# Strassen-Winograd sums taken in another order: S3 and T3 first and in place, one sum ahead of each product

## The chip, the cores and the metric

The kernel runs on one core of a Trainium2 chip. The metric is the device time of one execution in microseconds (us), lower is better; the time given for a kernel is the median of its runs. The engines are named as the profile names them: PE is TensorE's matmuls, PEld its weight loads, DVE is VectorE, ACT is ScalarE, POOL is GpSimd, SP is SyncE, which here issues nearly all transfers (DMA).

## The reference

One block of a streaming encoder on x of 1024 tokens by 1024 features, all in float32: a SwiGLU feed-forward, a mixing layer of two gated branches (retention and pooling), a second feed-forward.

```python
h = x + 0.5 * swiglu(rmsnorm(x, g1), w1_in, w1_out)          # 1024 -> 2 x 2816 -> 1024
u = rmsnorm(h, g2)
q, k, v, g_ret, p, gate_r, gate_p = split(u @ w_in)          # 1024 -> 7 x 1024
...                                                          # retention, pooling
merged = sigmoid(gate_r) * (ret @ w_ret_up) + sigmoid(gate_p) * (pool * scale)
h = h + merged @ w_out
h = h + 0.5 * swiglu(rmsnorm(h, g3), w2_in, w2_out)
out = rmsnorm(h, g)

def swiglu(x, w_in, w_out):
    gate, up = split(x @ w_in, 2)
    return (silu(gate) * up) @ w_out
```

## The kernel before

**A matrix product.** Every float32 number is split into a high part (a cast on ACT, L164, rounded to the matmul's format) and a low part (a subtraction on DVE, L165). One tile product is three matmuls, L184 (high by high), L185 and L186 (`mm3`). The low part of the moving weight is first read by L186, that of the operand by L185.

**A group.** Large products are done in groups of one 2x2 block of weights, with seven products in place of eight (Strassen-Winograd, function `strassen`). The weight blocks are L11, L12, L21, L22, the operand blocks R11, R12, R21, R22. The products are, with their numbers in the code, 0: L11·R11, 1: S2·T2, 2: S1·T1, 3: S3·T3, 4: L12·R21, 5: S4·R22, 6: L22·T4. The S are sums of weight blocks, the T of operand blocks. One product is 4 operand tiles of 128x512 with 3 matmuls each, so 12 matmuls. The two raw tiles of a group (`ra` with L11 and L12, `rb` with L21 and L22) are loaded by SP into a ring of 4 (`raw`). Sums that need a place of their own take a tile of a ring of 8 (`c2`). The split weight of one product is a tile of a ring of 5 (`wt`), named for its product: `wS1`, `wL22`.

**Results.** A group fills three banks: `a` (L11·R11, then + L12·R21), `b` and `e`. Product 0 goes into `a` and is copied by ACT into `b` (L529) before product 4 may add to `a`. Product 1 adds to `b`; ACT copies that to the tile `v` (L534) before product 2 may add to `b`. Product 3 goes into `e`, copied to `p7` (L551) before product 6 adds there. So in some orders PE waits for a copy that stands in ACT's row.

**Order.** `Flow.run` takes the products one after the other and prepares the weights (`prep_w`) four products ahead; behind each product it lets a few steps of background work run (operand sums, norms, gates). Groups run in pairs, A and B by turns. Where the operands are only just being made (the first pair of each feed-forward, the merge groups, w_out), the products follow `BY_OPERAND`. Engines run their instructions in the order of the program. Class `Next` makes the operands of the next stage: `r11`, `r21`, `r22`, `t1` to `t4_`, with the gain of the norm (`g`) folded in; there are four objects of it with such sums, `first` (first feed-forward), `mix` (the seven projections), `up` (retention's way up), and those of the output projection and the second feed-forward (made with `after`, which lists what each product needs).

**Names in the profile.** `a` and `a_..` are groups of the first feed-forward, `q0`, `k0`, `t1`, `p1` and so on of the projections, `ru0` to `ru3` of retention's way up, `wo0` to `wo3` of w_out, `c_..` of the second feed-forward. `n1T`, `ruT`, `mgT`, `n3T` are split T operands (in the listings of rows below `n1T12` is T1 of tile 2, `ruT40` T4 of tile 0), `n1R` and so on split R operands. `xs` are tiles of x in token order that ACT squares (L1147) for the first norm; `n1v` (L240), `n1r` (L241) are steps of its inverse root; `pg` (L1483) takes the pooling branch out of the two sum banks that `ru0b` and `ru1b` take next. `L390` and `L392` are the sums T4, `L359` T1, `L351` and `L353` T2 and T3, `L492` S1 and S2, `L505` S3, `L509` S4.

Of the kernel before, what the change touches and what calls it, by code (L numbers as in the profile page):

```python
# [15 lines left out]
ADD, SUB, MUL = ALU.add, ALU.subtract, ALU.mult  # L16
# [24 lines left out]
V_FFN1, V_MIX, V_FFN2, V_FINAL, V_SCALE, V_B0, V_B1, V_ONE = (i * KT for i in range(8))  # L41
# [9 lines left out]
N_MV, N_T4, N_RAW, N_WT, N_TL, N_C2 = 28, 9, 4, 5, 4, 8  # L51
LOOK = 4

BY_OPERAND = (0, 4, 1, 3, 2, 6, 5)


class Flow:
# [33 lines left out]
def block_kernel(ctx: ExitStack, tc, x, x_tok, x_two, vecs, f1_in, f1_out, w_in, w_v, pool_w, w_ret, w_pool, w_o,  # L91
# [3 lines left out]
    tt = nc.vector.tensor_tensor  # L95
    stt = nc.vector.scalar_tensor_tensor
# [3 lines left out]
    flow = Flow()  # L100
# [19 lines left out]
    def raw(name):  # L120
        return sb.tile([P, S], F32, tag="raw", bufs=N_RAW, name=name)
# [7 lines left out]
    def c2(name):  # L129
        return sb.tile([P, H], F32, tag="c2", bufs=N_C2, name=name)  # L130
# [4 lines left out]
    def sum_bank(name):  # L135

        return ps.tile([P, H], F32, tag="sum", bufs=N_SUM, name=name)

    def load(dst, src):
        nc.sync.dma_start(dst, src)  # L140
# [11 lines left out]
    def half(t, j):  # L152
        return t[:, j * H : (j + 1) * H]
# [22 lines left out]
    def weights(src, name, at=0):  # L176
        w = wt(name, at)
        n = src.shape[-1] // P
        split(flat(w, 0, n), flat(w, 1, n), src)
        return w  # L180
# [7 lines left out]
    def parts(m, at=slice(None)):  # L188
        return m[:, 0, at], m[:, 1, at]
# [31 lines left out]
    for n in range(N_SUM):  # L221
        b = sum_bank(f"set{n}")
# [57 lines left out]
    class Norm:  # L280
# [4 lines left out]
        def __init__(self, name):  # L285
            self.name, self.ssq, self.seen = name, None, set()
# [18 lines left out]
    class Next(Norm):  # L305

        turns = True

        def __init__(self, name, gain, keep=None):
            super().__init__(name)  # L310
            self.gain, self.keep = gain, keep
            self.M, self.Y, self.made, self.ready, self.tiles, self.t1s, self.rb = {}, {}, {}, set(), {}, {}, None
            self.t3s = set()
# [52 lines left out]
                self.t3s.add(i)  # L366

        def t2(self, i):
            self.sum1(i)
            R11, R22 = self.tiles[i, 0], self.tiles[i + 4, 1]  # L370
            self.less(R11, R22, self.t1s[i], i)
            self.put("T2", i, R11)

        def t1(self, i):
            self.put("T1", i, self.t1s[i], self.g(i))

        def t3(self, i):
            self.sum3(i)
            self.put("T3", i, self.tiles[i, 1])
# [98 lines left out]
    def strassen(nx, wa, wb, name, evac, end, begin=None, shared=(), dest=None):  # L478

        t = {}

        def blocks():
            ra, rb = raw(f"{name}ra"), raw(f"{name}rb")
            load(ra, wa)
            load(rb, wb)
            t.update(L11=half(ra, 0), L12=half(ra, 1), L21=half(rb, 0), L22=half(rb, 1))

        def combine(n, a, b, op):  # L490
            t[n] = c2(f"{name}{n}")
            tt(t[n], t[a], t[b], op)  # L492

        def prep_w(n):
            def go():
                if n == "L11":
                    blocks()
                elif n in ("S2", "S3") and "S1" not in t:
                    combine("S1", "L21", "L22", ADD)
                if n == "S2":  # L500
                    combine("S2", "S1", "L11", SUB)
                elif n == "S3":

                    t["S3"] = t["L21"]
                    tt(t["S3"], t["L11"], t["L21"], SUB)  # L505
                if n == "S4" or 3 in shared and n == "S1":

                    t["S4"] = t["S2"]
                    tt(t["S4"], t["L12"], t["S2"], SUB)  # L509
                t["w", n] = weights(t[n], f"{name}w{n}")  # L510

            return go

        def prod(dst, w, m, start, stop):
            for i in range(4):
                mm3(t[dst], parts(t["w", w], i), moving(nx.operand(m, i)), start and i == 0, stop and i == 3)

        def u(n):
            t[n] = c2(f"{name}{n}")
            return t[n]  # L520

        def b1():
            if begin:
                begin()
            t["a"] = bank(f"{name}a")
            prod("a", "L11", "R11", True, False)
            t["b"] = sum_bank(f"{name}b")
            with soon():
                copy(t["b"], t["a"])  # L529

        def b6():
            prod("b", "S2", "T2", False, False)
            with soon():
                copy(u("v"), t["b"])  # L534

        def fourth():

            if "b5" in t and "p7" in t:
                with soon():
                    evac((1, 1), t["b"], t["p7"])  # L540

        def b5():
            prod("b", "S1", "T1", False, False)
            t["b5"] = True
            fourth()

        def b7():
            t["e"] = bank(f"{name}e")
            prod("e", "S3", "T3", True, False)
            with soon():  # L550
                copy(u("p7"), t["e"])  # L551
            fourth()

        def b2():
            prod("a", "L12", "R21", False, True)
            with soon():
                evac((0, 0), t["a"], None)

        def b3():
            prod("b", "S4", "R22", False, True)  # L560
            with soon():
                evac((0, 1), t["b"], None)

        def b4():
            prod("e", "L22", "T4", False, True)
            with soon():
                evac((1, 0), t["e"], t["v"])

        def last(f):
            def go():  # L570
                f()
                t["ends"] = t.get("ends", 0) + 1
                if t["ends"] == 2:
                    end()

            return go

        g = Group([(prep_w("L11"), b1), (prep_w("S2"), b6), (prep_w("S1"), b5), (prep_w("S3"), b7),
                   (prep_w("L12"), b2), (prep_w("S4"), last(b3)), (prep_w("L22"), last(b4))])
        g.t, g.name, g.dest = t, name, dest  # L580
        g.finish = {3: last(lambda: evac((0, 1), t["b"], dest((0, 1)))), 2: lambda: evac((0, 0), t["a"], dest((0, 0)))}
        return g
# [168 lines left out]
    def ffn_in(nx, w, ops, name, ahead, start=None):  # L751
# [76 lines left out]
        if start:  # L828

            return chain(group(0), pairs_of_both(nx, (group(g) for g in order[1:]), BY_OPERAND, 3, ahead))  # L830
        return pairs_of_both(nx, (group(g) for g in order), BY_OPERAND, 2, ahead)

# [288 lines left out]
    first = Next("n1", V_FFN1)  # L1121
# [16 lines left out]
    quarters(1, range(4, 8))  # L1138
    load(cst, consts)
    flow.add(lambda: copy(ones_r, ones))  # L1140
    first.work(first.r11, first.r21, first.r12, first.r22, first.p22, first.t2, first.t3, first.t1, first.t4_)
    x_sums = eights("x_sums")

    def x_square(t):
# [9 lines left out]
    h1, h2 = spill("h1", KT), spill("h2", KT)  # L1154
# [17 lines left out]
        flow.rate = 2  # L1172
        yield from ffn_out(first, ops1, ops_done["a"], f1_out, x_two, "b", mix.quarter, end1, fetched)

    mix = Next("n2", V_MIX, h1)

    def end1(part):
        mix.work(*{2: (mix.r11,), 5: (mix.r22, mix.p22), 3: (mix.t2, mix.t1, mix.t3)}.get(part, ()))
# [551 lines left out]
    up = Next("ru", None)  # L1730
# [4 lines left out]
    def take(kts):  # L1735
        for kt in kts:
            r = t4(f"ret{kt}")
            load(r, ret[kt])
            up.tiles.update({(kt, j): half(r, j) for j in range(2)})
        if 7 in kts:  # L1740
            up.work(up.r22, up.t2, up.t1, up.t3, up.r21, up.p22, *[up.r22] * 3, up.t4_)
        else:
            up.work(up.r11)

# [47 lines left out]
    mg = Next("mg", None)  # L1792
    def after(nx):

        def t2(i):
            if i not in nx.t1s:
                nx.r22(i)
            nx.t2(i)

        return {0: nx.r11, 4: nx.r21, 1: t2, 3: nx.t3, 2: nx.t1, 6: nx.t4_, 5: nx.p22}  # L1800

    def two_groups(z):

# [76 lines left out]
    def handed(nx, last):  # L1880

        f = after(nx)

        def between(pair, n):
            if n in (3, 5):
                flow.add(*waiting)
                waiting.clear()
            if pair == 0:
                if n == BY_OPERAND[-1]:
                    flow.add(*(lambda m=m, i=i: m(i) for i in range(2) for m in (nx.r22, nx.sum1, nx.sum3)))  # L1890
                return
            flow.add(*(lambda i=i: f[n](i) for i in range(2)))

            for m in {3: (0,), 6: (4,)}.get(n, ()):
                flow.add(*(lambda i=i: f[m](i) for i in range(2, 4)))
            if n == BY_OPERAND[-1]:
                rest = [lambda m=m, i=i: f[m](i) for m in (1, 3, 2, 6, 5) for i in range(2, 4)]
                last(rest)

        return between  # L1900

    def merge():
        yield from two_by_two(two_groups(0) + two_groups(1), BY_OPERAND, handed(mg, lambda rest: flow.add(*rest)))
        yield from two_by_two((out_group(i) for i in range(4)), BY_OPERAND,
                              handed(ffn2, lambda rest: (flow.add(*rest[:4]), ffn2.stats(between=rest[4:]))))
# [198 lines left out]
```

## Time and profile before

| | |
|---|---|
| median of 3 runs | 2062.79 us (2062.39 to 2063.97) |
| the profiled execution | 2064.95 us, of which the span of the profile is 2063.2 us |
| granted TensorE clock | 0.999 |
| PE busy | 2043.0 us, 99% of the span |
| PEld busy | 1810.8 us, 88% |
| DVE busy | 1831.6 us, 89% |
| ACT busy | 1091.8 us, 53% |
| 16 DMA engines | 308 MB on the main queue, 44% |

A line of the timeline reads: start in us, duration in us, engine, line of the code and operation, out<-in (ring numbers left out), form, how many in a row, and in brackets the idle time of the engine just before and what ended it. A line of the waits reads: who waited, for whom, us in total, times, the longest. A line of the windows reads: the stretch, its length, then busy us and instructions of PE, PEld, DVE, ACT, POOL, then the granted clock, the share of the DMA engines and GB/s.

### The profile page before, as it was taken

To read this page: it belongs to the slowest core of one execution; us is meant where nothing else is said; L and a number is where in the kernel's file an instruction comes from. 1 tells how busy PE (TensorE), PEld (TensorE's weight loads), DVE (VectorE), ACT (ScalarE), POOL (GpSimd) and SP (SyncE) were. 2 spreads that over 40 slices of the span, in tenths; PEclk is the share of its full clock that TensorE was granted. 3 is DMA by queue.
4 is the path that set the end of the run, shared out by engine and by line. 5 is a ranking of instruction groups with operands and counts; after the bars stand their busy time and mean duration, and the time that the engine had idled before them with its cause. 6 is when DMAs were issued, how large, how long until landed. Compare 5 with 4: busy or idle time off the path is not lost.

```text
span 2063.2 us, 29735 instructions
## 1 busy us (share of the span) xinstructions
PE 2043.0 (99%) x10672; PEld 1810.8 (88%) x10672; DVE 1831.6 (89%) x3253; ACT 1091.8 (53%) x2064; POOL 9.0 (0%) x14
## 2 busy tenths in 40 slices
PE   9999999999999999999999999999999999999998
PEld 7888999988888888888888999888889999998887
DVE  8889898998996798989788888999989989899896
ACT  8545444554653554454447753457645545455454
POOL 0000000000000000000000000010000000000000
PEclk9999999999999999999999999999999999999999
DMA  6332424586543333243336566645223232367642
GB/s 244 137 103 77 143 87 143 200 272 197 188 144 101 114 131 115 82 153 118 118 138 231 190 223 224 237 106 169 82 91 132 93 136 88 134 208 273 212 146 100
DMA packets 120260, 313.57 MB, mean 152 GB/s; under 512 B 13361, under 2 KB 17585, under 8 KB 120113
## 3 DMA queue, kind: packets, MB, share of 16 engines
q1 hardware_dynamic: 118096, 308.01, 44.0%
q0 software_dynamic: 1440, 2.62, 0.9%
q8 instruction: 83, 1.36, 0.3%
q10 hardware_dynamic: 576, 1.05, 0.1%
q14 instruction: 65, 0.52, 0.1%
HBM read 220.93 MB, written 90.70 MB: 151 GB/s over the span
## 4 chain that ended last, share of the span: by engine, by line
PE 84%; DVE 9%; DMA 3%; ACT 3%; issue 1%; SPq 0%; ACTq 0%; DVEq 0%
PE c_b L184 2%; PE c_b L185 2%; PE c_b L186 2%; PE a_b L184 2%; PE a_b L186 2%; PE a_b L185 2%; PE c_e L186 2%; PE c_e L184 2%; PE c_e L185 2%; PE a_e L186 2%; PE a_e L184 2%; PE a_e L185 2%; PE a_a L186 1%; PE a_a L185 1%; PE a_a L184 1%
## 5 line engine op out<-in xcount | busy, mean ns | idle before, releaser
L184 PE MATMUL c_b<-n3T,c_wS 128*128 128x512 f32 x176 | 66.8, 380 | 1.7 <-ACT n3T L164 1.7
L185 PE MATMUL c_b<-n3T,c_wS 128*128 128x512 f32 x176 | 66.8, 380 | 0.0
L186 PE MATMUL c_b<-n3T,c_wS 128*128 128x512 f32 x176 | 66.7, 379 | 0.0
L184 PE MATMUL a_b<-n1T,a_wS 128*128 128x512 f32 x168 | 63.7, 379 | 0.0
L185 PE MATMUL a_b<-n1T,a_wS 128*128 128x512 f32 x168 | 63.7, 379 | 0.0
L186 PE MATMUL a_b<-n1T,a_wS 128*128 128x512 f32 x168 | 63.7, 379 | 0.0
L184 PE MATMUL a_a<-n1R,a_wL 128*128 128x512 f32 x120 | 45.5, 379 | 0.0
L185 PE MATMUL a_a<-n1R,a_wL 128*128 128x512 f32 x120 | 45.5, 379 | 0.0
L186 PE MATMUL a_a<-n1R,a_wL 128*128 128x512 f32 x120 | 45.5, 379 | 0.0
L184 PE MATMUL c_a<-n3R,c_wL 128*128 128x512 f32 x112 | 42.7, 381 | 0.7 <-ACT c_b L529 0.5
L185 PE MATMUL c_a<-n3R,c_wL 128*128 128x512 f32 x112 | 42.4, 379 | 0.0
L186 PE MATMUL c_a<-n3R,c_wL 128*128 128x512 f32 x112 | 42.4, 379 | 0.0
L184 PEld LDWEIGHTS c_b<-n3T,c_wS 128*128 128x128 f32 x176 | 33.3, 189 | 6.7 <-ACT n3T L164 2.1
L185 PEld LDWEIGHTS c_b<-n3T,c_wS 128*128 128x128 f32 x176 | 33.3, 189 | 4.8 <-DVE n3T L165 0.3
L186 PEld LDWEIGHTS c_b<-n3T,c_wS 128*128 128x128 f32 x176 | 33.3, 189 | 4.7
L186 PEld LDWEIGHTS a_b<-n1T,a_wS 128*128 128x128 f32 x168 | 31.8, 189 | 4.5
L184 PEld LDWEIGHTS a_b<-n1T,a_wS 128*128 128x128 f32 x168 | 31.8, 189 | 4.4
L185 PEld LDWEIGHTS a_b<-n1T,a_wS 128*128 128x128 f32 x168 | 31.8, 189 | 4.4
L165 DVE TENSOR_TENSOR a_wS<-a_S,a_wS 128x512 fp32r<-128x512 f32 x45 | 31.0, 690 | 3.6 <-ACT a_wS L164 3.6
L165 DVE TENSOR_TENSOR c_wS<-c_S,c_wS 128x512 fp32r<-128x512 f32 x46 | 31.7, 690 | 2.6 <-ACT c_wS L164 2.6
L164 ACT CAST a_wS<-a_S 128x512 fp32r<-128x512 f32 x45 | 27.4, 621 | 11.8 <-PE a_a L186 6.1
L184 PE MATMUL c_e<-n3T,c_wS 128*128 128x512 f32 x88 | 33.5, 380 | 0.0
(3165 smaller groups left out, 8025.3 us busy)
## 6 DMA issues: line engine op xcount, KB each, us to landing
c_ra<-in_f_in SPq DMA_DIRECT2D x22, 512.0 KB, 3.7
c_rb<-in_f_in SPq DMA_DIRECT2D x22, 512.0 KB, 3.6
a_ra<-in_f_in SPq DMA_DIRECT2D x21, 512.0 KB, 3.8
a_rb<-in_f_in SPq DMA_DIRECT2D x21, 512.0 KB, 3.7
t<-au SPq DMA_DIRECT2D x11, 512.0 KB, 3.0
b<-ag SPq DMA_DIRECT2D x11, 512.0 KB, 4.2
r<-au SPq DMA_DIRECT2D x11, 512.0 KB, 3.7
bra<-in_f_out SPq DMA_DIRECT2D x11, 512.0 KB, 5.1
```

The costliest lines, as they stand in the source:

```text
L164: copy(hi, src)
L165: tt(lo, src, hi.bitcast(F32), SUB)
L184: mm(dst, w[0], m[0], start=start, stop=False, skip_group_check=True)
L185: mm(dst, w[0], m[1], start=False, stop=False, skip_group_check=True)
L186: mm(dst, w[1], m[0], start=False, stop=stop, skip_group_check=True)
```

## The change

Weights: S3 = L11 - L21 is made first, in L11's place; then S2 = L22 - S3 in the same place, S1 = L21 + L22 in L21's place, S4 = L12 - S2 in S2's place. There are four sums of 128x512 for each group as before, but each product now has one of its own ahead of it (before, S1 and S2 were made together ahead of the first of them), and none takes a tile of `c2`. So `ra` holds S4 until it has been split.

Operands of `first`, `up`, of w_out and of the second feed-forward: T3 = R12 - gR22 in place, T2 = gR11 + T3 in place, T1 = R22 - T2 in a `c2` tile. There are three sums for each tile as before. T1 is now a plain split (L164, L165) in place of a scaled one (L168, L169). `mix` keeps the old sums.

Order: `BY_OPERAND` has product 3 (S3·T3) ahead of product 1 (S2·T2), and the lists of operand work follow it.

```diff
-BY_OPERAND = (0, 4, 1, 3, 2, 6, 5)
+BY_OPERAND = (0, 4, 3, 1, 2, 6, 5)
...
         def t2(self, i):
-            self.sum1(i)
             R11, R22 = self.tiles[i, 0], self.tiles[i + 4, 1]
-            self.less(R11, R22, self.t1s[i], i)
+            if self.by_t3:
+                self.sum3(i)
+                T3 = self.tiles[i, 1]
+                if self.gain is None:
+                    tt(R11, R11, T3, ADD)
+                else:
+                    stt(R11, R11, self.g(i), T3, MUL, ADD)
+            else:
+                self.sum1(i)
+                self.less(R11, R22, self.t1s[i], i)
             self.put("T2", i, R11)
 
         def t1(self, i):
-            self.put("T1", i, self.t1s[i], self.g(i))
+            if self.by_t3:
+                R22, T2 = self.tiles[i + 4, 1], self.tiles[i, 0]
+                t1 = c2(f"{self.name}t1{i}")
+                tt(t1, R22, T2, SUB)
+                self.put("T1", i, t1)
+            else:
+                self.put("T1", i, self.t1s[i], self.g(i))
...
-                elif n in ("S2", "S3") and "S1" not in t:
-                    combine("S1", "L21", "L22", ADD)
-                if n == "S2":
-                    combine("S2", "S1", "L11", SUB)
                 elif n == "S3":
-
-                    t["S3"] = t["L21"]
+                    t["S3"] = t["L11"]
                     tt(t["S3"], t["L11"], t["L21"], SUB)
+                elif n == "S2":
+                    t["S2"] = t["S3"]
+                    tt(t["S2"], t["L22"], t["S3"], SUB)
+                elif n == "S1":
+                    t["S1"] = t["L21"]
+                    tt(t["S1"], t["L21"], t["L22"], ADD)
...
-    first.work(first.r11, first.r21, first.r12, first.r22, first.p22, first.t2, first.t3, first.t1, first.t4_)
+    first.work(first.r11, first.r21, first.r12, first.r22, first.p22, first.t3, first.t2, first.t1, first.t4_)
...
-    mix = Next("n2", V_MIX, h1)
+    mix = Next("n2", V_MIX, h1, False)
...
-            up.work(up.r22, up.t2, up.t1, up.t3, up.r21, up.p22, *[up.r22] * 3, up.t4_)
+            up.work(up.r22, up.t3, up.t2, up.t1, up.r21, up.p22, *[up.r22] * 3, up.t4_)
...
-        return {0: nx.r11, 4: nx.r21, 1: t2, 3: nx.t3, 2: nx.t1, 6: nx.t4_, 5: nx.p22}
+        return {0: nx.r11, 4: nx.r21, 1: nx.t2, 3: t3, 2: nx.t1, 6: nx.t4_, 5: nx.p22}
```

Three places show what this does to the rows of the engines. The line numbers of the changed kernel are 8 to 15 higher for the same step (L529 becomes L541, L534 L546, L1147 L1159, L390 L405).

The first is ACT in the first pair of the first feed-forward (groups `a11` and `a1`), at the casts of T1 (`n1T10` to `n1T13`). Before:

```order
L164 CAST n1T33_621<-x3_95 128x512
L168 ACTIVATE n1T10_641<-n1t10_471,vec_66 128x512
L534 COPY a11_v_614<-a11_b_519 128x512
L164 CAST a1_wS1_624<-a1_S1_527 128x512
L168 ACTIVATE n1T11_644<-n1t11_493,vec_66 128x512
L168 ACTIVATE n1T12_665<-n1t12_521,vec_66 128x512
L168 ACTIVATE n1T13_668<-n1t13_549,vec_66 128x512
L534 COPY a1_v_639<-a1_b_547 128x512
```

And after:

```order
L1159 ACTIVATE xs6_809,x_sums_123<-xs6_809 128x1024
L1159 ACTIVATE xs7_812,x_sums_123<-xs7_812 128x1024
L563 COPY a1_p7_629<-a1_e_616 128x512
L164 CAST a11_wL22_641<-a11_rb_394 128x512
L788 COPY ag1_579<-a1_a_522 128x512
L164 CAST n1T10_633<-n1t10_631 128x512
L164 CAST n1T11_638<-n1t11_636 128x512
L546 COPY a11_v_656<-a11_b_512 128x512
L164 CAST a1_wL22_668<-a1_rb_421 128x512
L241 ACT_TABLE_LOAD
L241 ACTIVATE n1r0_832<-n1v_831 128x8
L164 CAST n1T12_660<-n1t12_658 128x512
```

The casts of T1 now stand behind the last squares of `xs` and, from `n1T12` on, behind the load of the root's table; before, they stood ahead of both.

The second is ACT in the projections, at the copy `t1v` of group `t1` (`p1ws..` are weights that the pair p1, t1 shares). Before:

```order
L164 CAST p1wx3_7151<-p1S2_7037 128x512
L1257 ACTIVATE t0z11_7148<-t0B_6890,vec_66 128x512
L164 CAST p1ws123_7157<-p1s123_7154 128x512
L551 COPY t1p7_7173<-t1e_7160 128x512
L164 CAST p1ws343_7177<-p1S2_7037 128x512
L534 COPY t1v_7192<-t1b_7055 128x512
```

And after:

```order
L1269 ACTIVATE t0z11_7098<-t0B_6844,vec_66 128x512
L563 COPY t1p7_7123<-t1e_7110 128x512
L164 CAST p1wx3_7101<-p1ra_6874 128x512
L164 CAST p1ws123_7107<-p1s123_7104 128x512
L546 COPY t1v_7142<-t1b_7006 128x512
```

The copy `t1v` no longer stands behind the second shared cast, `p1ws343`.

The third is ACT in the first pair of retention's way up, at the copy `ru1b`. Before:

```order
L529 COPY ru0b_12965<-ru0a_12952 128x512
L164 CAST ru1wS2_12979<-ru1S2_12977 128x512
L529 COPY ru1b_12999<-ru1a_12986 128x512
L164 CAST ru0wS3_13010<-ru0rb_12770 128x512
L164 CAST ruT40_13192<-ret4_12612 128x512
L164 CAST ruT41_13199<-ret5_12614 128x512
```

And after:

```order
L164 CAST ru1wS3_12881<-ru1ra_12720 128x512
L164 CAST ruT40_13098<-ret4_12522 128x512
L164 CAST ruT41_13105<-ret5_12524 128x512
L541 COPY ru1b_12901<-ru1a_12888 128x512
L164 CAST ru0wS2_12914<-ru0ra_12679 128x512
```

The casts of two T4 operands moved ahead of the copy `ru1b`. The sums that they wait for stand on DVE, after, as follows (L1495 is `pg`, L405 T4):

```order
L1495 TENSOR_TENSOR pg70_12648<-pu7d0_12765,pg70_12648 128x512
L1495 TENSOR_TENSOR pg71_12649<-pu7d1_12766,pg71_12649 128x512
L165 TENSOR_TENSOR ru0wS3_12839<-ru0ra_12679,ru0wS3_12839 128x512
L517 TENSOR_TENSOR ru1rb_12721<-ru1rb_12721 128x512
L514 TENSOR_TENSOR ru0ra_12679<-ru0rb_12680,ru0ra_12679 128x512
L405 TENSOR_TENSOR ret4_12522<-ret4_12522,ret0_12514 128x512
L405 TENSOR_TENSOR ret5_12524<-ret5_12524,ret1_12516 128x512
```

The second sum T4 is the fifth row behind `pg`, which in the kernel before was all that the copy `ru1b` waited for.

More of the change, by code (lines that the diff above doesn't have):

```diff
@@ L307, in block_kernel, with __init__ @@
         turns = True
-        def __init__(self, name, gain, keep=None):
+        def __init__(self, name, gain, keep=None, by_t3=True):
             super().__init__(name)
+            self.by_t3 = by_t3
             self.gain, self.keep = gain, keep
@@ L488, in blocks @@
             t.update(L11=half(ra, 0), L12=half(ra, 1), L21=half(rb, 0), L22=half(rb, 1))
-        def combine(n, a, b, op):
-            t[n] = c2(f"{name}{n}")
-            tt(t[n], t[a], t[b], op)
         def prep_w(n):
@@ L1793, in after, with t3 @@
     def after(nx):
-        def t2(i):
-            if i not in nx.t1s:
+        def t3(i):
+            if i not in nx.t3s:
                 nx.r22(i)
-            nx.t2(i)
-        return {0: nx.r11, 4: nx.r21, 1: t2, 3: nx.t3, 2: nx.t1, 6: nx.t4_, 5: nx.p22}
+            nx.t3(i)
+        return {0: nx.r11, 4: nx.r21, 1: nx.t2, 3: t3, 2: nx.t1, 6: nx.t4_, 5: nx.p22}
     def two_groups(z):
@@ L1884, in between @@
         def between(pair, n):
-            if n in (3, 5):
+            if n in (1, 5):
                 flow.add(*waiting)
@@ L1889, in between @@
                 if n == BY_OPERAND[-1]:
-                    flow.add(*(lambda m=m, i=i: m(i) for i in range(2) for m in (nx.r22, nx.sum1, nx.sum3)))
+                    flow.add(*(lambda m=m, i=i: m(i) for i in range(2) for m in (nx.r22, nx.sum3)))
                 return
             flow.add(*(lambda i=i: f[n](i) for i in range(2)))
-            for m in {3: (0,), 6: (4,)}.get(n, ()):
+            for m in {1: (0,), 6: (4,)}.get(n, ()):
                 flow.add(*(lambda i=i: f[m](i) for i in range(2, 4)))
             if n == BY_OPERAND[-1]:
-                rest = [lambda m=m, i=i: f[m](i) for m in (1, 3, 2, 6, 5) for i in range(2, 4)]
+                rest = [lambda m=m, i=i: f[m](i) for m in (3, 1, 2, 6, 5) for i in range(2, 4)]
                 last(rest)
```

## Prediction

> **What bounds the kernel.** I read the page's busy times first, then what PE waited for, then the timeline around each of those waits. The busy times:
>
> ```profile
> PE 2043.0 (99%) x10672; PEld 1810.8 (88%) x10672; DVE 1831.6 (89%) x3253; ACT 1091.8 (53%) x2064; POOL 9.0 (0%) x14
> ```
>
> PE is the bound, and neither its matmuls nor their shapes change. So time moves only through the 20.2 us of the 2063.2 us span in which PE is idle, or through new idle time. From the list of PE's waits, those at steps that the change touches:
>
> ```profile
> PE c_b L184 <- ACT n3T L164: 1.7, 1, 1.7
> ...
> PE t1b L184 <- ACT t1v L534: 0.9, 1, 0.9
> ...
> PE ru1a L184 <- ACT ru1b L529: 0.8, 1, 0.8
> ...
> PE wo0e L186 <- DVE wo0wS L165: 0.2, 1, 0.2
> ...
> PE t1e L186 <- DVE t1wS L165: 0.2, 1, 0.2
> ```
>
> With wo2a (1.2) and c_a (0.5) below they make 5.5 us; each costs some 0.3 us more than its gap, which counts from the end of the matmul before (0.38 long, though the next normally starts 0.22 behind it, by 165.41 us for 759 matmuls in the stretch below), and the first one after it takes 0.48. About 7.5 us is therefore all that can be won. Slower has no such bound. The difference that a measurement of this kernel can tell from none is 0.2%, 4.1 us.
>
> **Cost of the sums themselves.** Four weight sums a group before and after, three operand sums a tile: 0.6 us of DVE each (two of `pg` below take 1.28, each 0.69 long), the same number. T1's split loses a scale, which shortens it on both engines if anything (a scaled cast is 0.65 below, a plain one 0.62): nothing. What counts is order, and a place for place walk of the new rows with the old durations gives four terms.
>
> **Term 1, first feed-forward, first pair: +2.1 us.** T1 is now made last, from T2, and the casts of `n1T10` to `n1T13` stand behind the squares of `xs`.
>
> ```profile
> L140 SPq DMA_DIRECT2D xs<-in_x_tok x8: 328/328/384, 16.8 to 50.9; - x8
> L1147 ACT ACTIVATE xs<-xs x8: 1044/1056/1072, 27.1 to 55.7; 128x1024 f32<-128x1024 f32 x8
> ...
> DMA to landing us min/median/max: 3.5/4.0/8.6
> ```
>
> ```profile
> 43.75 1.95 ACT L168 ACTIVATE n1T<-n1t,vec 128x512 fp32r<-128x512 f32 x3
> 57.37 1.28 ACT L241 ACT_TABLE_LOAD   x1
> 50.48 0.38 PE L184 MATMUL a_b<-n1T,a_wS 128*128 128x512 f32 x1
> ```
>
> Before, T1 was cast by 45.7, 4.8 us before PE's third T1 tile at 50.48; the last square came at 55.7. After, all eight squares stand ahead. Two `xs` tiles alternate, so a square comes no sooner than the square two back, plus 1.1 for that square, plus a landing of 3.5 to 4.0: about 5 us a step. The first stands at 28.1 (27.1, and two T3 casts now ahead of it; casts and copies of ACT follow each other by 0.5, as three do from 741.03 to 742.55 below), so the seventh is at 43.3 and the eighth, one square and a short wait behind, at 45.3, ending at 46.4. Behind it two copies and a cast (1.5), two T1 casts (1.0), the copy `a11_v` and a cast (1.0), the table (1.28) and the root (0.2): `n1T12` is cast from 51.4 to 52.0. PE, held 0.26 by the copy `a11_v`, wants it at 50.7 and loses 1.3; DVE's low part follows at 52.7, when L185 would stand at 52.2: 0.5 more. Ends: 0, if the loads land at once, and 4, if each of three steps takes 0.6 more. I take 2.1, with the median landing.
>
> **Term 2, projections, t1: -1.2 us.** ACT, DVE and PE there:
>
> ```profile
> 736.41 0.69 DVE L165 TENSOR_TENSOR t1wS<-t1S,t1wS 128x512 fp32r<-128x512 f32 x1 [0.85 <-ACT t1wS L164]
> 738.66 0.69 DVE L165 TENSOR_TENSOR t1wS<-t1S,t1wS 128x512 fp32r<-128x512 f32 x1 [0.35 <-ACT t1wS L164]
> 740.52 0.42 DVE L593 TENSOR_TENSOR p1s<-p1s,p1S 128x256 f32<-128x256 f32 x1
> 741.03 0.62 ACT L164 CAST p1ws<-p1s 128x512 fp32r<-128x512 f32 x1 [0.40 <-DVE p1s L593]
> 742.55 0.59 ACT L534 COPY t1v<-t1b 128x512 f32<-128x512 f32 x1
> 743.19 0.48 PE L184 MATMUL t1b<-n2T,t1wS 128*128 128x512 f32 x1 [0.90 <-ACT t1v L534]
> ```
>
> After, the two half sums follow the split of 738.66 directly (done at 740.0, not 740.9), and the copy stands right behind the cast `p1ws123`: 740.6 to 741.1, before PE is free at 742.1. That takes back 1.2 us. The S3 split that `t1e` waited for stands two rows earlier on DVE, which would be 0.4 more; but late next is the S2 split of t1 at 736.41, whose cast stands behind the same rows of ACT as before, and PE would wait for that instead. Ends: 0 and -1.6; I take -1.2, for the rows leave nothing else in the copy's way.
>
> **Term 3, retention's way up: +4.2 us at ru1a, then given back.**
>
> ```profile
> 1311.77 1.28 DVE L1483 TENSOR_TENSOR pg<-pu7d,pg 128x512 f32<-128x512 f32 x2
> 1312.54 0.57 ACT L529 COPY ru1b<-ru1a 128x512 f32<-128x512 f32 x1 [0.58 <-DVE pg L1483]
> 1317.29 0.62 ACT L164 CAST ruT<-ret 128x512 fp32r<-128x512 f32 x1 [3.65 <-DVE ret L390]
> 1313.16 0.48 PE L184 MATMUL ru1a<-ruR,ru1wL 128*128 128x512 f32 x1 [0.76 <-ACT ru1b L529]
> ```
>
> Before, ACT copied `ru1b` and then waited 3.65 us for T4. After, two T4 casts stand ahead of the copy. With `pg` where it was, DVE's next rows are a split (1312.97), S1, S2 and two T4 sums, the last from 1315.4 to 1316.1; ACT casts it until 1316.7 and copies until 1317.3. PE goes on at 1317.3, not 1313.16: 4.15 us. Queued behind the copy on ACT are only splits that PE wants after that. Ends: 0 (if T4 were ready) and 5 (if DVE is two sums later there).
>
> **Term 4, w_out and the start of the second feed-forward: -4.9 us.**
>
> ```profile
> 1300.00:1470.00 170.00, 165.41 (x759) 142.39 (x758) 165.07 (x271) 101.16 (x180) 8.84 (x10) 1.00 0.49 149
> ```
>
> ```profile
> 1320.18 0.69 DVE L1837 TENSOR_TENSOR ru0h<-ru0a,rg 128x512 f32<-128x512 f32 x1
> 1419.42 0.68 DVE L492 TENSOR_TENSOR wo2S<-wo2S,wo2ra 128x512 f32<-128x512 f32 x1
> 1420.19 0.62 ACT L164 CAST wo2wS<-wo2S 128x512 fp32r<-128x512 f32 x1 [1.41 <-PE wo3a L186]
> 1421.35 0.48 PE L184 MATMUL wo2a<-mgR,wo2wL 128*128 128x512 f32 x1 [1.24 <-ACT wo2b L529]
> 1458.42 0.48 PE L184 MATMUL c_a<-n3R,c_wL 128*128 128x512 f32 x1 [0.54 <-ACT c_b L529]
> 1468.15 0.48 PE L184 MATMUL c_b<-n3T,c_wS 128*128 128x512 f32 x1 [1.74 <-ACT n3T L164]
> ```
>
> In this stretch DVE is as full as PE, 165 of 170 us, and PE's waits are DVE's lateness handed on: the copy `wo2b` stood behind the cast of S2, whose sum ended at 1420.11 (the PE row in that bracket is the last of several semaphores, but `wo3a` had nothing to do with the sum). After, the first sum, S3, stands about nine rows earlier, and the wait goes (-1.5). DVE's splits run a few rows ahead of PE, and its evacuation of `ru0a` at 1320.18 stood 8 us behind PE, which had ended that product by 1312.4 (ru1a's 1313.16 less the gap), so 4.2 us of PE's delay at ru1a does not delay DVE: PE arrives later at wo0e, c_a and c_b (0.4, 0.8 and 2.1 with the spread matmuls), and finds them ready. DVE by itself delivers the low T3 part that the second feed-forward waits for at 1467.7; PE without waits, 4.8 less and 4.2 more than before, wants it at 1468.3. So terms 3 and 4 make -0.7 together; without the delay at ru1a the same place would be DVE's, at -1.0. Ends: +4.2, if DVE is delayed with PE, and -4.9. I take -0.7, since both ways of counting meet there.
>
> **What I cost at nothing.** The `ra` tile is held until S4 and its half sums are split.
>
> ```profile
> 1651.00 0.33 SPq L140 DMA_DIRECT2D c_ra<-in_f_in  x1
> ...
> 1659.80 0.69 DVE L165 TENSOR_TENSOR c_ws<-c_S,c_ws 128x512 fp32r<-128x512 f32 x1 [0.41 <-ACT c_ws L164]
> ...
> 1668.52 0.68 DVE L165 TENSOR_TENSOR c_wL<-c_ra,c_wL 128x512 fp32r<-128x512 f32 x1
> ```
>
> ```profile
> c_ra<-in_f_in SPq DMA_DIRECT2D x22, 512.0 KB, 3.7
> ```
>
> The next pair's first load was issued at 1651.0; after, it waits for the split of 1659.8, goes out at 1660.5, lands after 3.7 at 1664.2, and is first split at 1668.5: 4.3 us to spare. If that cover were gone, every pair would lose what is missing. The diagonal of the second norm's spread (`n20b`) and T1 of tiles 2 and 3 in the second feed-forward come within 0.5 us of PE: +0.2 for both.
>
> **The sum.** +2.1 - 1.2 - 0.7 + 0.2 = +0.4 us on the profiled execution. That execution took 2064.95 us, 2.2 above the median of the runs; I apply the difference to the median: 2063.2 us.
>
> **A rule of the skill against this.** At ru1a PE would be idle for 5.0 us, where its longest idle time now is 1.7 at a granted clock of 1.00. The Trainium skill, "TensorE: Matmul & The Clock Gate", Part 1 on the clock gate, says that an idle window of about 3.4 us halves the array's clock until it has been busy as long. No row here shows it. By the page's figure some 1.7 us would be added, an estimate, and the sum would be 2064.9.
>
> **Rivals.**
> *The held tiles make loads late* (slower). The rows for it: SP issues in order, and DVE already waits for `c_ra` in the timeline of each pair. Against it: 4.3 us to spare. It decides once a landing takes over 8 us, against 3.7. With 22 groups, 11 pairs, in this feed-forward and as many in the first, 0.4 us a pair would be 8.8 us, and with my sum 2072.0. Chance 0.12.
> *The delays add and nothing comes back* (slower): DVE's evacuations wait on PE after ru1a, so the waits of w_out and c_b stay. +2.1 - 1.2 + 4.2 + 0.2 = +5.3: 2068.1. The point is whether DVE's idle time between 1320 and 1400 grows. Chance 0.10.
> *The delays do not come* (faster): DVE is ahead at T4 and the squares land early, while term 4 holds with DVE's limit loosened by the smoother sums: -1.2 - 4.9 = -6.1: 2056.7; it must win c_b's 2.1 too to pass 4.1. Chance 0.12.
> *PE runs at half pace after the idle 5 us*: one product of 12 matmuls at 0.44, not 0.22, us: +2.6, 2065.8. Chance 0.08.
> *The delay of term 1 fails to come, the rest holds* (the loads land while ACT is busy anyway): -1.7, 2061.1. Chance 0.13.
> My forecast, between 2061.5 and 2065: 0.45.
>
> **Numbers.** Faster by over 0.2%: 0.12. Slower: 0.20, the first two rivals less the mild end of the second. The rest, 0.68, is the same. The range takes in the second rival and most of the third: 2057.8 to 2068.4.
>
> **What the profile after would show.** Term 1: a wait of a_b for `n1T` of 1.5 to 2 us near 51. Term 2: no row t1b <- t1v. Term 3: ru1a <- ru1b near 5 us. Term 4: no wait at wo2a, and none over 1 us at c_a and c_e or c_b. I am wrong if groups beyond the first pairs show PE waits for weights, or DVE waits for `ra` longer than before.

## Result and the profile after

The changed kernel takes 2073.33 us (median of 6 runs, 2070.26 to 2075.35); the kernel before, run beside it, 2063.97 us (median of 6, 2062.39 to 2064.91). The ratio is 1.0046, with a 95% interval of 1.0036 to 1.0056: slower by 9.4 us, where 2063.2 us and a range up to 2068.4 us had been predicted.

The page's busy times of the changed kernel; the profiled execution took 2070.26 us, its fastest, with a span of 2068.5 us:

```profile
PE 2044.4 (99%) x10672; PEld 1810.2 (88%) x10672; DVE 1835.1 (89%) x3253; ACT 1092.7 (53%) x2064; POOL 9.1 (0%) x14
```

The same instructions, nearly the same busy times, and PE idle for 24.1 us instead of 20.2. What PE waited for at the steps in question (total us, times, longest):

```profile
PE ru1a L184 <- ACT ru1b L541: 3.1, 1, 3.1
...
PE c_e L185 <- DVE n3T L165: 1.0, 2, 0.7
PE a_b L184 <- ACT n1T L164: 1.0, 1, 1.0
PE a_b L184 <- ACT a_v L546: 1.0, 1, 1.0
...
PE dp6b L185 <- DVE dp6m L165: 0.6, 2, 0.4
PE bp6b L185 <- DVE bp6m L165: 0.6, 2, 0.4
...
PE c_a L184 <- ACT c_b L541: 0.5, 1, 0.5
...
PE wo0b L186 <- DVE wo0wS L165: 0.5, 1, 0.5
PE wo1b L186 <- DVE wo1wS L165: 0.4, 1, 0.4
PE t1b L186 <- DVE t1wS L165: 0.4, 1, 0.4
```

wo2a, t1b at the copy, and c_b at `n3T` are gone, as forecast (`n3T` is now waited for by c_e); a_b and ru1a are there, as forecast. bp6b and dp6b, the second products of the two down projections, are new, and stood nowhere in the prediction. What DVE waited for shows why:

```profile
DVE ds L931 <- DMA dL22a<-in_f_out: 2.4, 1, 2.4
...
DVE bs L931 <- DMA bL22a<-in_f_out: 2.0, 1, 2.0
```

At T1 near 50 and at ru1a the rows behind PE's waits are these (ACT first, then PE):

```profile
46.51 1.06 ACT L1159 ACTIVATE xs<-xs 128x1024 f32<-128x1024 f32 x1 [1.53 <-DMA xs<-in_x_tok]
52.60 1.12 ACT L164 CAST n1T<-n1t 128x512 fp32r<-128x512 f32 x2
53.26 0.48 PE L184 MATMUL a_b<-n1T,a_wS 128*128 128x512 f32 x1 [0.99 <-ACT n1T L164]
```

```profile
1315.28 1.22 ACT L164 CAST ruT<-ret 128x512 fp32r<-128x512 f32 x2 [4.13 <-DVE ret L405]
1316.41 0.58 ACT L541 COPY ru1b<-ru1a 128x512 f32<-128x512 f32 x1
1317.04 0.48 PE L184 MATMUL ru1a<-ruR,ru1wL 128*128 128x512 f32 x1 [3.05 <-ACT ru1b L541]
```

The two traces have the same matmuls in nearly the same order, so I set the n-th matmul of one beside the n-th of the other and read how much later PE is. From place to place its lateness changes so:

| place (us, before) | change of PE's lateness, us |
|---|---|
| start, to 48 | +0.4 |
| first feed-forward, T1 (48 to 92) | +3.0 |
| rest of its up and gate groups | -0.3 |
| change to its down projection (416 to 459) | +1.5 |
| projections, t1 (715 to 756) | -1.2 |
| retention's products (`ob`, `s`: 1136 to 1258) | -1.6 |
| ru1a (1313) | +2.1 |
| w_out and start of the second feed-forward | -0.7 |
| its up and gate groups | +0.2 |
| change to its down projection (1832 to 1914) | +2.0 |
| sum (before rounding, with the small steps left out here) | +5.3 |

That is the difference of the spans, 5.3. The medians differ by 9.4: the profiled execution of the kernel before lies 1.0 above its median, that of the changed kernel 3.1 below its own, and something more had to be found.

### The profile page after: what moved, and what is told of

Same layout as the page of the kernel before. It is cut to its first block, busy times and chain, and to the rows that moved or that the text cites. A ratio compares the mean times of both kernels' runs of the same rounds, so it can differ in the third digit from the quotient of the medians.

```text
span 2068.5 us, 29758 instructions
## 1 busy us (share of the span) xinstructions
PE 2044.4 (99%) x10672; PEld 1810.2 (88%) x10672; DVE 1835.1 (89%) x3253; ACT 1092.7 (53%) x2064; POOL 9.1 (0%) x14
## 4 chain that ended last, share of the span: by engine, by line
PE 69%; DVE 18%; DMA 5%; issue 4%; ACT 4%; SPq 0%; POOL 0%; ACTq 0%; DVEq 0%; POOLq 0%
PE c_b L184 2%; PE c_b L185 2%; PE c_b L186 2%; PE a_b L185 2%; PE a_b L186 2%; PE a_b L184 2%; PE c_e L185 1%; PE a_e L186 1%; PE c_e L186 1%; PE a_e L184 1%; PE a_e L185 1%; PE c_e L184 1%; PE a_a L186 1%; PE a_a L185 1%; PE a_a L184 1%
## 5 line engine op out<-in xcount | busy, mean ns | idle before, releaser
L164 ACT CAST a_wS<-a_ra 128x512 fp32r<-128x512 f32 x45 | 27.6, 618 | 24.3 <-DVE a_ra L514 11.5
L164 ACT CAST c_wS<-c_ra 128x512 fp32r<-128x512 f32 x46 | 28.3, 619 | 16.5 <-DVE c_ra L514 12.5
L184 PE MATMUL c_e<-n3T,c_wL 128*128 128x512 f32 x88 | 33.4, 380 | 0.0
```

Source lines behind the costliest of these rows:

```text
L164: copy(hi, src)
L184: mm(dst, w[0], m[0], start=start, stop=False, skip_group_check=True)
```

## Experiments

All were run beside the kernel before, in three groups (runs 1 to 4, 5 to 8, 9 and 10); its medians there were 2063.49, 2063.84 and 2063.90 us. Diffs are against the changed kernel unless said otherwise.

**1. The changed kernel again** (no edit).

> The changed kernel once more. Its profiled run lost 5.3 us to the kernel before, its median 9.4, and its runs spread over 5 us against 2.5. Theory A (loads that have lost their cover: the first bL22a and dL22a, the xs tiles): the spread stays, 2070 to 2075, and another trace shows PE's waits at a_b near 50, bp6b, dp6b and ru1a with other lengths and no new place. Theory B (the array's clock, after PE's 3 us at ru1a): a slow run's trace shows a stretch with a granted clock below 1.00 behind ru1a and the waits themselves as before.

2072.71 us (2069.72 to 2075.15), ratio 1.0042 (1.0029 to 1.0055). The waits for the loads had the lengths of the first trace (2.0 and 2.1 us), and the trace of this run, 2.4 us longer, has a stretch at half pace behind ru1a. Its windows (us; PE, PEld, DVE, ACT, POOL busy; granted clock; DMA share; GB/s):

```profile
1314.00:1318.00 4.00, 1.18 (x6) 0.70 (x6) 4.00 (x8) 2.25 (x4) 0.00 (x0) 1.00 0.47 155
1318.00:1320.00 2.00, 2.00 (x7) 1.62 (x6) 2.00 (x4) 0.31 (x1) 0.00 (x0) 0.58 1.05 385
1320.00:1322.00 2.00, 2.00 (x6) 1.61 (x6) 2.00 (x4) 1.06 (x3) 0.00 (x0) 0.56 0.85 257
1322.00:1324.00 2.00, 2.00 (x11) 1.73 (x11) 2.00 (x5) 0.38 (x1) 0.00 (x0) 1.00 0.57 220
```

Six or seven matmuls in 2 us instead of eleven, at a granted clock of 0.58 and 0.56, and then full speed again; eight matmuls stand some 0.43 us apart instead of 0.22, which costs 1.6 us. Theory B is right about the stretch, though its condition was too strict: the wait was 2.8 us here, shorter than the 3.1 us that left the clock alone in the first trace. Theory A, in so far as it made the loads vary from run to run, is not borne out.

**2. T1 and T2 of the first norm as before.**

```diff
-    first = Next("n1", V_FFN1)
+    first = Next("n1", V_FFN1, None, False)
-    first.work(..., first.t3, first.t2, first.t1, first.t4_)
+    first.work(..., first.t2, first.t3, first.t1, first.t4_)
```

> The changed kernel with the first norm's T1 and T2 made as before (T1 from R12 - R11, T2 from it), so that the T1 casts stand ahead of the last four squares and of the table load. Theory (term 1): PE's waits at a_b near 50 to 54 go, 2.8 to 3.0 us less, and the rest of the trace stays. Rival (given back: PE meets a later wait, such as the vL one at 613 or bp6b, a little longer): under 1.5 us.

2072.27 us (2070.38 to 2075.62), ratio 1.0045 (1.0032 to 1.0058). In its trace the three gaps at a_b shrink by 1.14, 1.15 and 0.51 us, so 2.8 as the theory has it; then 1.8 us go to half pace behind ru1a, and more to longer waits elsewhere (a_b at 82 us 0.75, `ob` and `s` together 1.2, c_y 0.55, c_x 0.84), so that this trace is 2.0 us longer than the first one of the changed kernel. The medians show a gain of 0.4. By itself this run doesn't tell the theory from the rival; runs 7 and 8 do.

**3. S2 and S4 in a tile of their own.**

```diff
-                    t["S2"] = t["S3"]
+                    t["S2"] = c2(f"{name}S2")
                     tt(t["S2"], t["L22"], t["S3"], SUB)
```

> The changed kernel with S2 and S4 in a tile of their own, so that ra is free again after S3 and L12, as early as before; all else stays. Theory A: the first bL22a goes out near 382, not 395, DVE's waits for it (1.95 and 2.4 us) go, and PE's waits at bp6b, dp6b and the c_x before it: 2.8 to 3.3 us less by the trace, more by the median if the spread comes from there too (4 to 6). Rival (the waits at bp6b come from the last group's gating, which is later on DVE whatever the loads do): the load is early and less than 1 us is gained.

2069.99 us (2069.60 to 2071.24), ratio 1.0033 (1.0020 to 1.0045). The first `bL22a` load, by the rows of the tile (issue times, first to last), in the kernel before, and then in the changed one:

```profile
L140 SPq DMA_DIRECT2D bL22a<-in_f_out x11: 328/378/948, 381.9 to 440.4; - x11
```

```profile
L140 SPq DMA_DIRECT2D bL22a<-in_f_out x11: 328/333/528, 395.1 to 446.2; - x11
```

and with S2 apart:

```profile
L140 SPq DMA_DIRECT2D bL22a<-in_f_out x11: 328/378/950, 383.6 to 442.1; - x11
```

13 us late in the changed kernel, it is out at 383.6 here and keeps nobody waiting: DVE's two waits for L22a are gone, and so are all of PE's at bp6b and dp6b (1.2 and 0.9 us of lateness) and 0.3 at the c_x ahead of dp6b. At the two changes of stage PE is 3.1 us earlier than in the changed kernel, as the theory has it. The same trace had 4.4 us of idle time at ru1a, 2.9 us lost at half pace, and a new wait of 2.5 us at t6b (every trace with S2 apart everywhere has one there; run 8 has its cause), so that it is 1.0 us longer than the first one. The gain of 2.7 by the medians lies by the theory's 2.8 to 3.3, but with five executions each it is not clear of zero; what shows the mechanism are the rows of the load and of the waits.

**4. The T4 casts behind the copy ru1b.** Two sums T4 read a zero made from ru1b, so nothing can put them ahead of it; one small instruction more. For this the T4 steps leave `up`'s list of operand work and are added behind the first product of the pair.

```diff
+        def t4_behind(i):
+            if i == 0:
+                act(up.none, made[1].t["b"][:, :1], AF.Copy, scale=0.0)
...
+            if i < 2:
+                stt(R21, R21, up.none, T2, ADD, SUB)
+                up.put("T4", i, R21)
```

> The changed kernel with the first two T4 sums of retention's way up made to depend on the copy ru1b (a zero taken from a column of it is added), so that the two casts stand behind it on ACT. The wait at ru1a falls from 3.05 to 0.8 us. As predicted (the delay is given back, since DVE sets the time at c_e and c_b): the end moves by 0.3 us or less, and the waits near 1400 and 1470 grow by 2. Rival (not given back): 2.3 us less at the end.

2068.75 us (median of 11, 2065.90 to 2070.37), ratio 1.0023 (1.0014 to 1.0032): 4.0 us below run 1. The traces say where: the wait at ru1a is gone, PE is 3.5 us earlier behind it than in the changed kernel (0.2 of that it was ahead of it), 2.9 behind c_e, and 3.3 at the end. Next to nothing is given back, so my prediction of that is refuted. The windows from 1313 us on, of the changed kernel first, with DVE the third busy time:

```profile
1313.00:1330.00 17.00, 13.95 (x65) 11.91 (x64) 15.25 (x25) 7.74 (x14) 0.00 (x0) 1.00 0.73 240
1330.00:1350.00 20.00, 20.00 (x95) 17.50 (x94) 17.76 (x30) 6.39 (x12) 0.00 (x0) 1.00 0.54 176
1350.00:1370.00 20.00, 20.00 (x94) 17.53 (x93) 17.99 (x31) 12.11 (x23) 1.88 (x2) 1.00 0.36 80
```

```profile
1313.00:1330.00 17.00, 17.00 (x80) 14.91 (x79) 16.75 (x28) 9.01 (x18) 0.00 (x0) 1.00 0.73 242
1330.00:1350.00 20.00, 20.00 (x94) 17.50 (x94) 19.58 (x34) 7.34 (x14) 0.00 (x0) 1.00 0.51 176
1350.00:1370.00 20.00, 20.00 (x95) 17.46 (x94) 17.84 (x30) 10.42 (x19) 2.74 (x3) 1.00 0.43 101
```

DVE does 3.2 us less work in these 57 us when PE has stood still at ru1a. It waits for ACT and PE, and ACT for PE's later products; in the changed kernel's rows (ACT, then DVE twice):

```profile
1330.29 0.59 ACT L546 COPY ru1v<-ru1b 128x512 f32<-128x512 f32 x1 [1.49 <-PE ru1b L186]
```

```profile
1331.43 0.69 DVE L165 TENSOR_TENSOR ru0wS<-ru0ra,ru0wS 128x512 fp32r<-128x512 f32 x1 [1.90 <-ACT ru0wS L164]
1332.88 0.69 DVE L1843 TENSOR_TENSOR ru0h<-ru0b,ru0p 128x512 f32<-128x512 f32 x1 [0.76 <-PE ru0b L186]
```

The cast that the first of DVE's rows waits for stands right behind that copy on ACT. DVE is late by as much afterwards: the low T3 part that c_e waits for, of the changed kernel and of this one:

```profile
1469.25 0.68 DVE L165 TENSOR_TENSOR n3T<-wo,n3T 128x512 fp32r<-128x512 f32 x1
```

```profile
1466.31 0.69 DVE L165 TENSOR_TENSOR n3T<-wo,n3T 128x512 fp32r<-128x512 f32 x1
```

2.9 us apart, and c_e waits 0.7 and 0.3 us for it in both.

**5. Operand sums and order of products alone** (weight sums of the kernel before; the changed kernel's `prep_w` replaced by that one).

> The kernel before with the operand sums and the order of products of the changed one; the weight sums stay as they were (S1, S2 in tiles of their own, S3 in L21). bL22a goes out early here, and no T4 cast stands ahead of the copy ru1b, so only T1's wait near 50 is left of the changed kernel's losses. Theory (the loss comes from the weight sums, but for T1's 3 us): 2064 to 2067, with a spread of some 2.5 us and no stretch at half pace. Rival (the operand sums themselves cost more, by other waits): 2068 or more.

2069.55 us (median of 7, 2067.67 to 2070.75), ratio 1.0028 (1.0017 to 1.0039). The time is the rival's, but neither theory nor rival named what the trace shows, a wait of the first pair of the way up one product earlier:

```profile
1315.35 0.80 PE L184 MATMUL ru0a<-ruR,ru0wL 128*128 128x512 f32 x1 [5.49 <-ACT ru0b L544]
```

```profile
1310.39 0.62 ACT L164 CAST ruT<-rut 128x512 fp32r<-128x512 f32 x1 [7.13 <-DVE rut L387]
...
1314.72 0.58 ACT L544 COPY ru0b<-ru0a 128x512 f32<-128x512 f32 x1
```

```profile
1309.06 0.69 DVE L507 TENSOR_TENSOR ru1S<-ru1rb 128x512 f32<-128x512 f32 x1 [4.73 <-DMA ru1rb<-in_w_ret]
```

It is the same mechanism with other tiles. DVE stood 4.7 us at a weight sum whose load had not landed; the T1 sums, now last, were queued behind it; ACT stood at their casts; and the copy `ru0b` stood behind those. 5.5 us, and half pace behind it (2.1). In the rest of the trace little is lost, not even at T1 near 50, where two of its casts stand ahead of the last square here. So the losses of the two halves don't add up to that of the whole: which cast stands ahead of which copy is another in each.

**6. Weight sums and order of products alone** (all norms' operand sums as before, `by_t3=False`).

> The changed kernel with every norm's operand sums made as before (T1 from R12 - R11, T2 from it), so that only the weight sums and the order of products differ. Theory: T1's wait is gone, the late bL22a and dL22a, the wait of 3 us at ru1a and the half pace behind it in some runs are all there: 2068 to 2071, spread 4 us or more. Rival (the loss is in the operand sums): within 2 us of the kernel before.

2073.32 us (2069.90 to 2075.54), ratio 1.0045 (1.0033 to 1.0058). All that was expected is in the trace: no wait at a_b for `n1T`; bp6b and dp6b with 0.6 us each; 4.0 us at ru1a, and half pace behind it (1.7). The median is 2 us above what I gave. c_a waits 2.7 us here, against 0.5; why, I didn't follow up.

**7. Both mends of the weight sums' side**: the edits of runs 3 and 4.

> The changed kernel with both mends of the weight sums' side: S2 and S4 in a tile of their own, and the T4 casts behind the copy ru1b. Theory: the early loads narrow the spread (1.6 us in the kernel with S2 apart) and the clock stays at 0.999: 2070.0 less 4.4 of ru1a's wait and 2.5 of half pace, so 2063 to 2065, spread under 2.5 us. Rival (time given back at c_e and c_b or before): 2067 or more.

2065.15 us (median of 11, 2063.55 to 2069.41), ratio 1.0010 (1.0001 to 1.0019). By time this is 0.15 above the theory's range and well below the rival's; the spread is not under 2.5, and neither is that of the kernel before beside it (2061.25 to 2066.03 in 23 runs), so the spread says nothing.

**8. All three mends**: the edit of run 2 added.

> The same with the first norm's T1 made as before too. Theory: 2 to 3 us below the one without it, 2060 to 2063, at or a little below the kernel before, with no wait of PE above 2.5 us. Rival (the 3 us are given back, as they nearly were in the run that had this mend alone: 0.4 by the medians): the same as without it, 2063 to 2065.

2062.99 us (median of 11, 2061.01 to 2064.72), ratio 0.9994 (0.9985 to 1.0003). T1 is worth 2.2 us by the medians, not given back, and the whole loss is undone. Against the kernel before it is the same within the measurement. Its longest waits:

```profile
PE t6b L184 <- ACT t6v L546: 1.7, 1, 1.7
PE set L225 <- DVE zero L220: 1.2, 1, 1.2
PE vL L185 <- DVE vL11w L165: 1.1, 1, 1.1
```

t6b is not in the kernel before; runs 3 and 7 have it too (2.5 and 1.7). The loads of group p0 go out just ahead of the stores of `t5z`, as in the kernel before, and the stores land 5.0 instead of 3.2 us after; ACT waits 2.7 us for them, with the copy `t6v` behind.

**9. The three mends, S2 apart in the last pairs only.**

```diff
-                    t["S2"] = t["S3"]
+                    t["S2"] = c2(f"{name}S2") if name in ("a10_", "a21_", "c10_", "c21_") else t["S3"]
```

> As the kernel with all three mends, but S2 has a tile of its own only in the last pair of each feed-forward's up and gate groups, the pair whose ra tiles the first bL22a and dL22a take over; all other groups hold ra as in the changed kernel. Theory (only the change of stage pays for the held tile): no wait of PE at bp6b or dp6b, and the p0 loads, late again, leave the stores of t5z alone, so that t6b's wait of 1.7 us goes: 2061 to 2062.5, below the kernel before. Rival (the held tiles cost a little in every pair, which the medians saw and one trace did not): 2064 to 2066.

2064.15 us (median of 11, 2061.99 to 2069.66), ratio 1.0002 (0.9993 to 1.0011). The waits at t6b and, for L22a, at bp6b and dp6b are gone as expected, but the time is not below the kernel before: c_y and c_b, in the middle of the second feed-forward, cost 1.0 us, and the first down projection waits 1.5 us for evacuations. Those stand on DVE behind a wait of 4.3 us for another load of that projection, `bL` (2.7 at most in the kernel before). By time the run lies at the lower edge of the rival's range.

**10. That edit alone in the changed kernel.**

> The changed kernel with nothing but that: S2 apart in the last pair of each feed-forward's up and gate groups. Theory: the same gain as with S2 apart everywhere, 2 to 3.5 us below the changed kernel, 2069 to 2071, with a spread under 3 us. Rival (held tiles cost in every pair): within 1 us of the changed kernel, 2072 to 2073.

2071.48 us (2070.38 to 2073.16), ratio 1.0035 (1.0023 to 1.0048): 1.2 to 1.9 us below the changed kernel's two medians and 0.5 above the theory's range, with both of DVE's waits for L22a gone. In its trace the first change of stage costs 1.1 us less and the second 0.9 less (with 1.0 of new waits there), while ru1a takes 1.4 more and half pace 1.7. So the last pairs pay for a part of what the held tile costs. By the rows of the traces it is most of it, but the medians of runs 9 and 10 leave room for a microsecond or more in the other pairs; that is not settled.

## Why the prediction was wrong

By the medians of runs 1, 4, 7 and 8, which mend one thing after another, 4.0 us go with the T4 casts, 3.6 with the held tile and 2.2 with T1: 9.7, from 2072.71 to 2062.99. Each of the three steps is clear of zero (drawing the executions anew, 95% of the differences lie in 1.0 to 6.4, 1.3 to 4.6 and 1.2 to 4.0); the gains of one mend alone in runs 2, 3 and 10 are not. In the first trace, where +0.4 was forecast and +5.3 came, 0.9 of the difference is term 1, 2.1 are terms 3 and 4, 3.5 the changes of stage, and retention gave 1.6 back. The terms one by one:

- **Term 1** (T1 behind the squares): +2.1 was forecast; 3.0 in the trace, 2.2 by the medians. The mechanism was right, and the eighth square was at 46.5 where I had 45.3: by my own rule it hung on the sixth, which ended at 41.8, and its load landed at 46.4, but I let it follow the seventh. The term was short because the copy `a11_v`, behind the first T1 casts, cost 1.1 (I took 0.3), counted from start to start as I had counted. The wait for `n1T` and DVE's low part made 1.65, near my 1.8; the first matmuls behind the three waits add 0.3.
- **Term 2** (t1): -1.2 forecast and -1.2 in the trace.
- **Term 3** (ru1a): the order was read rightly: two T4 sums end at 1315.9, the casts follow, the copy goes out at 1316.4 and PE goes on at 1317.0; I had 1316.7 and 1317.3. PE waited 3.1 in the first trace, 2.3 more than before, and 2.8 to 4.5 in the others where the casts stand ahead of the copy. I had 4.15 more, with PE on time; it came 1.6 late, and the size was fair.
- **Term 4, the first step that failed**: "4.2 us of PE's delay at ru1a does not delay DVE". I judged by one product, `ru0a`, which PE had ended 8 us before DVE came to it. But DVE's list behind it holds other work that needs PE's later products, and an engine that is busy for 165 of 170 us can't make up what it then loses: it idled 3.2 us more and delivered `n3T` 2.9 us later (run 4). Of the 4.9 us that I had coming (4.8 by its parts), wo2a's 1.4 came; c_b's 1.9 came back as 1.7 at c_e, and wo1b and wo0b took 1.4. Terms 3 and 4 together gave +1.4, not -0.7. The prediction's second rival, at 0.10, had named this test.
- **"What I cost at nothing", the second step that failed**: I looked for the next user of the held `ra` within the same loop, found `c_ra` with 4.3 us to spare, and stopped. No pair did lose much in the trace: DVE waits 1.0 us for `ra` and `rb` there in all, where it waited 17.0 in the kernel before. But behind the last pair the same four tiles go to the down projection's `bL22a` and `L12`, whose first load was 13 us late. With 1.5 and 2.0 us at the two changes of stage (3.6 by the medians) it is the first rival's mechanism, but at two places rather than 22.
- **The rival of half pace**, at 0.08 and +2.6: it came in the traces of all runs with a wait of 2.8 us or more at this place but one, with 1.6 to 2.9 us. It deserved more than half: the rule of the Trainium skill was quoted with the right price (1.7 us), and then counted as a rival because no row of the kernel before showed it, where none could, with 1.7 us as its longest wait. It is also the largest thing found of what the medians show beyond the first trace: run 1's trace, which lies at its median, is 2.4 us longer than the first, and half pace costs it 1.6. The 1.0 us by which the kernel before's own trace lies above its median is not explained.
- **Not foreseen**: 1.6 us won at `ob` and `s` in retention. In other traces of these kernels they come out between nothing and 1.6; I did not look for the cause.

## What to carry to other kernels

A buffer that is held longer has to be followed around its ring beyond the loop, to the first tile of the next stage; what it delays there has no cover from the loop's rhythm. Of a queue that runs in order, the question is which short instruction on the critical path (here the copy of a sum bank) now stands behind one that waits for a slow engine; moving sums around changes that everywhere, and a wait of 3 us can cost half as much again by the clock. A delay is given back only where the engine that sets the end has idle time of its own to catch up in; here, at 97% busy, it had none to speak of.

## What the runs showed of the hardware

In six of seven traces the array fell to half pace around an idle time of PE of 2.8 us or more, in one it did not. Idle time before the first matmul at ru0a or ru1a, and what the slower matmuls behind it cost beyond 0.22 us each:

| run | idle, us | cost of half pace, us |
|---|---|---|
| changed kernel, first trace | 3.05 | 0 |
| 1 (again) | 2.82 | 1.6 |
| 2 (T1 as before) | 2.95 | 1.8 |
| 6 (weight sums alone) | 4.0 | 1.7 |
| 3 (S2 apart) | 4.40 | 2.9 |
| 10 (S2 apart in the last pairs) | 4.5 | 1.7 |
| 5 (operand sums alone) | 5.49 | 2.1 |

Idle times of 2.5 (t6b in run 3) and 2.7 us (c_a in run 6) were followed by full speed. The Trainium skill ("TensorE: Matmul & The Clock Gate", Part 1) gives an idle window of about 3.4 us, running freely, so that the point of change varies; idle times of 2.82 and 2.95 us were enough here. The cost does not grow with the idle time, as it would not with a window that runs freely; the usual cost is that of some 3.4 us at half speed, as the Trainium skill has it, and run 3's 2.9 is more. Nor is the change tied to the end of the wait: in run 1 it came some 1 us after PE had gone on, and in run 3 the granted clock stood at 0.84 from 1316 to 1318 us, where PE was still idle until 1318.5. The first matmuls of every trace stand 0.43 us apart too, in the kernel before from 1.2 to 5.5 us, and there the granted clock reads 1.00. Where the bound lies between, or whether the little work around the idle time counts too, these runs don't tell.

How often it comes can be guessed from the mean granted clock of every execution, which 3.4 us at half speed in 2070 us would lower by 0.001. It is 0.998 or lower in 32 of 38 executions of the kernels in the table, in 7 of 44 with the T4 casts behind the copy (runs 4, 7, 8 and 9), and in 6 of 53 of the kernel before beside them. That does not say where in an execution the clock fell.
